# Output projection of a hybrid decoder layer: eight products of quarters replaced by seven (Strassen, Winograd's form)

## Chip, cores and metric

One core of a Trainium2 chip runs the kernel. The metric is the device time of one execution in microseconds (us); lower is better. The text calls the engines by the profile's names: PE is TensorE (PEld its weight loads), DVE is VectorE, ACT is ScalarE, POOL is GpSimd, SP is the engine whose queue issues every DMA.

## The reference

One decoder layer on a sequence of 1024 tokens with 1024 features, in float32. Three groups of heads work side by side; their gated results are concatenated to `y` (1024 x 1024) and projected by `w_out` (1024 x 1024). The result is normalized over its 1024 features, gated and added to the input:

```python
h = rmsnorm(x, g_pre) * (1.0 + scale[:, None]) + shift[:, None]
proj = h @ w_in
...
y_m = mlstm_branch(...) * jax.nn.silu(mz)
y_a = swa_branch(aq, ak, av, a_sinks) * jax.nn.silu(az)
y_s = stickbreak_branch(sq, sk, sv) * jax.nn.silu(sz)
y = jnp.concatenate([y_m, y_a, y_s], axis=-1) @ w_out
return x + gate[:, None] * rmsnorm(y, g_post)
```

## The kernel before, in words

Products that need float32 accuracy are made with split operands. `split` (L68) copies a float32 tile to a high part in the matmul's own format (ACT, L70) and subtracts to get a low part (DVE or POOL, L71). A product then takes three matmuls: high x high, low x high, high x low. `hh` and `hl` hold the high and low parts of the feature-major input, eight chunks `k` of 128 features by 1024 tokens. For most of the kernel that input is `h`, which the 128-feature blocks of the input projection read (`ProjD`, L359). These blocks are also the filler: `fill` issues their matmuls one by one between the steps of the mLSTM, the sliding window and the stick-breaking attention, so that PE always has something to do. The last of the blocks are the gates `z`.

`gated` (L468) handles a gate block when it is complete. It takes the sigmoid (ACT), multiplies the block by the group's result (DVE, L473), then by the sigmoid (POOL, L484, one step later), and one step after that (`rest`) splits the finished 128 x 512 piece of `y` and stores both parts in DRAM (`d_yh`, `d_yl`, L482 and L483). Chunks 6 and 7 (the stick-breaking heads) stay in SBUF (`ys`) and are split late, straight into `hh` and `hl`.

When the attention is done its SBUF is given back and the output stage begins (L1068). `wo_load` (L1072) loads a 128 x 1024 row block of `w_out` and splits it into `woh` and `wol`; `y_load` (L1077) runs the late splits of one half of the tokens and loads the stored parts of `y` back into `hh` and `hl`, over the old input, as soon as the last gate block has read it. `out_mm` (L1102) does one chunk for a 128-token row tile `i` and a half `n` of the columns, three matmuls of 128 x 512 into one PSUM bank (L1107 to L1109). Four row tiles advance together over seven chunks (eight banks), then they are completed one by one, and the other four row tiles follow, each over all eight chunks. `out_fin` (L1111) finishes a row tile: squares with a sum (ACT, L1120), multiplication by the gate row `gbc` from PSUM (DVE, L1122 and L1125), the power -1/2 (POOL, L1124), and per half a last operation with the reloaded `x` (DVE, L1128) and a store.

PE's order is that of the program text (`manual_schedule`, L74). The order on DVE, ACT, POOL and SP is chosen when the kernel is built, from program order and the readiness that the build's own timing gives; at run time each engine and SP's queue runs strictly in that order. Buffers rotate per tag (`bufs`): a new tile of a tag waits until the last reader of the tile that had the buffer is done.

Of the kernel before, what the change touches and what calls it, by code (L numbers as in the profile page):

```python
# [10 lines left out]
F32 = mybir.dt.float32  # L11
F32R = mybir.dt.float32r
# [34 lines left out]
def trunk(ctx: ExitStack, tc, x, w_ss, w_gate, rows, cols, w_mu, w_mif, w_dm, w_av, wqk, bif, alibi, w_out,  # L47
# [61 lines left out]
    d_yh, d_yl = dram("d_yh", [KT, P, S]), dram("d_yl", [KT, P, S])  # L109

    h_stk = ExitStack()
    hp = pool("ht", stack=h_stk)
# [355 lines left out]
    def gated(dst_j, name):  # L468
        def f(ps, n, t, src):
            sg = gst.tile([P, 512], F32, tag="gs", bufs=2, name=f"gs_{name}{n}")  # L470
            A.activation(sg, ps, AF.Sigmoid)
            y = src
            V.tensor_tensor(out=y, in0=ps, in1=src, op=ALU.mult)  # L473
# [10 lines left out]
            later(1, lambda: G.tensor_tensor(out=y, in0=y, in1=sg, op=ALU.mult))  # L484
            later(2, rest)
        return f
# [578 lines left out]
    ka_stk.close()  # L1065


    wop = pool("wop", side="right", stack=g_stk)  # L1068
    woh = wop.tile([P, KT, D], F32R, name="woh")
    wol = wop.tile([P, KT, D], F32R, name="wol")  # L1070

    def wo_load(k):  # L1072
        w = wop.tile([P, D], F32, tag="wo", bufs=2, name=f"wo{k}")
        load(w, w_out[k])
        split(woh[:, k, :], wol[:, k, :], w, A.copy, V if k % 2 else G)

    def y_load(n):  # L1077

        t = slice(n * 512, (n + 1) * 512)
# [20 lines left out]
    pso = {}  # L1100

    def out_mm(i, n, k):  # L1102
        t, cs = slice(i * P, (i + 1) * P), slice(n * 512, (n + 1) * 512)
        if k == 0:
            pso[i, n] = fbank(f"op{i}_{n}") if i % 4 == 3 else ops_.tile([P, 512], F32, tag="op", name=f"op{i}_{n}")
        o = pso[i, n]
        T.matmul(o, hh[:, k, t], woh[:, k, cs], start=(k == 0), stop=False)  # L1107
        T.matmul(o, hl[:, k, t], woh[:, k, cs], start=False, stop=False)  # L1108
        T.matmul(o, hh[:, k, t], wol[:, k, cs], start=False, stop=(k == KT - 1))  # L1109

    def out_fin(i):  # L1111
        t = slice(i * P, (i + 1) * P)
        xr = op_.tile([P, D], F32, tag="xr", bufs=2, name=f"xr{i}")
        load(xr, x[t, :])
        st = op_.tile([P, 4], F32, tag="st", bufs=2, name=f"st{i}")
        ot = op_.tile([P, D], F32, tag="ot", bufs=2, name=f"ot{i}")
        for n in range(2):
            cs = slice(n * 512, (n + 1) * 512)
            sj = op_.tile([P, 512], F32, tag="sj", bufs=2, name=f"sj{i}_{n}")
            A.activation(sj, pso[i, n], AF.Square, accum_out=st[:, n:n + 1])  # L1120
            if n == 0:
                V.tensor_tensor(out=ot[:, cs], in0=pso[i, n], in1=gbc[:, cs], op=ALU.mult)  # L1122
        V.tensor_scalar(out=st[:, 2:3], in0=st[:, 1:2], scalar1=st[:, 0:1], scalar2=D * EPS, op0=ALU.add, op1=ALU.add)  # L1123
        G.tensor_tensor(out=st[:, 3:4], in0=st[:, 2:3], in1=mhalf[:, 0:1], op=ALU.pow)  # L1124
        V.tensor_tensor(out=ot[:, 512:D], in0=pso[i, 1], in1=gbc[:, 512:D], op=ALU.mult)  # L1125
        for n in range(2):
            cs = slice(n * 512, (n + 1) * 512)
            V.scalar_tensor_tensor(out=ot[:, cs], in0=ot[:, cs], scalar=st[:, 3:4], in1=xr[:, cs], op0=ALU.mult,  # L1128
                                   op1=ALU.add)
            store(out[t, cs], ot[:, cs])  # L1130
        del pso[i, 0], pso[i, 1]

    for k in range(KT - 1):
        for i in range(4):
            for n in range(2):
                out_mm(i, n, k)
    for i in range(NT):
        for n in range(2):
            for k in ([KT - 1] if i < 4 else range(KT)):
                out_mm(i, n, k)  # L1140
        out_fin(i)
    for stack in (o_stk, g_stk, h_stk, fps_stk):
        stack.close()

# [47 lines left out]
```

## Time and profile before

| | |
|---|---|
| median of 3 runs | 552.52 us (552.3 to 553.77) |
| the profiled execution | 553.0 us, span 551.2 us |
| mean granted PE clock | 0.997 |
| PE busy | 523.9 us, 95%, 2953 matmuls |
| DVE busy | 332.5 us, 60% |
| ACT busy | 250.3 us, 45% |
| POOL busy | 220.6 us, 40% |
| three groups of output matmuls (L1107, L1108, L1109) | 128 each |

Busy times are of the one profiled execution. Matmuls overlap in the pipeline, so the duration of a row on PE is longer than the step from one matmul to the next. An arrow `<-` in a row's last field names what ended the idle time before it. A row of DMA on `SPq` is the time of its issue, not of its transfer.

### The profile page before, as it was taken

What the parts mean: (1) busy time and instruction counts of PE and PEld (TensorE: products, weight loads), DVE (VectorE), ACT (ScalarE), POOL (GpSimd) and SP (SyncE); (2) the same over time, 40 slices, a digit from 0 to 9 for tenths busy, and PEclk for the clock granted to TensorE, in tenths of its full rate; (3) what the DMA queues carried; (4) which work ended last, traced back from release to release, by engine and by line L of the source; (5) the groups of instructions that cost most, each with busy time, mean ns of one, the idle gap of its engine ahead of it and who ended that gap; (6) DMA issues with size and microseconds to landing.
All of it is one profiled execution on the core that took longest, in us unless ns stands there. A gap on an engine that the chain in (4) does not pass through costs nothing.

```text
span 551.2 us, 8550 instructions
## 1 busy us (share of the span) xinstructions
PE 523.9 (95%) x2953; PEld 449.0 (81%) x2953; DVE 332.5 (60%) x750; ACT 250.3 (45%) x571; POOL 220.6 (40%) x206
## 2 busy tenths in 40 slices
PE   4799999999998999999998999899999999999995
PEld 3577899899987989888786888788888888888884
DVE  4686692053707887678887479787878442108232
ACT  5643533451113333267677568667668432213100
POOL 2365765420033343234534348574766433111000
PEclk9999999999999999999999999999999999999998
DMA  8982360247986455699843389455421169607421
GB/s 307 417 293 75 120 227 21 59 145 219 284 240 222 135 162 125 162 268 299 238 150 98 125 226 249 142 149 167 134 77 59 39 193 404 238 5 238 144 84 69
DMA packets 63659, 96.57 MB, mean 175 GB/s; under 512 B 17600, under 2 KB 36992, under 8 KB 63488
## 3 DMA queue, kind: packets, MB, share of 16 engines
q1 hardware_dynamic: 63616, 96.03, 54.8%
q8 instruction: 23, 0.38, 0.3%
q14 instruction: 20, 0.16, 0.1%
HBM read 69.24 MB, written 25.20 MB: 171 GB/s over the span
## 4 chain that ended last, share of the span: by engine, by line
PE 78%; DVE 10%; DMA 4%; ACT 3%; issue 2%; POOL 2%; SPq 1%; DVEq 0%; POOLq 0%; ACTq 0%
PE pd L359 24%; PE ptav L385 6%; PE mu L233 6%; PE op L1109 5%; PE op L1108 5%; PE op L1107 5%; PE tp L994 3%; DMA ka<-d_akl 3%; PE ptmif L385 2%; DVE cu L509 2%; PE ops L1012 2%; PE ops L1013 2%; PE xps L166 2%; PE z L963 2%; PE mr L197 1%
## 5 line engine op out<-in xcount | busy, mean ns | idle before, releaser
L359 PE MATMUL pd<-hh,wl_d 128*128 128x512 f32 x256 | 71.1, 399 | 0.0
L359 PE MATMUL pd<-hh,wh_d 128*128 128x512 f32 x256 | 70.6, 400 | 0.0
L359 PE MATMUL pd<-hl,wh_d 128*128 128x512 f32 x256 | 70.6, 398 | 0.0
L302 POOL TENSOR_TENSOR wl_d<-w_d,wh_d 128x512 fp32r<-128x512 f32 x32 | 44.0, 1398 | 29.1 <-ACT wh_d L300 19.6
L359 PEld LDWEIGHTS pd<-hh,wh_d 128*128 128x128 f32 x256 | 46.1, 188 | 8.4 <-issue 0.5
L359 PEld LDWEIGHTS pd<-hl,wh_d 128*128 128x128 f32 x256 | 46.1, 188 | 8.0
L359 PEld LDWEIGHTS pd<-hh,wl_d 128*128 128x128 f32 x256 | 45.8, 188 | 7.7
L1108 PE MATMUL op<-woh,hl 128*128 128x512 f32 x128 | 50.6, 396 | 0.0
L1109 PE MATMUL op<-wol,hh 128*128 128x512 f32 x128 | 50.6, 396 | 0.0
L1107 PE MATMUL op<-woh,hh 128*128 128x512 f32 x128 | 50.6, 396 | 0.0
L982 POOL TENSOR_TENSOR sg<-sg,pr 128x512 f32<-128x512 f32 (+1 forms) x30 | 31.1, 1041 | 20.8 <-DVE pr L980 20.6
L857 POOL TENSOR_SCALAR zb<-zb,mx 128x256 f32<-128x256 f32 (+1 forms) x24 | 21.6, 914 | 42.5 <-DVE mx L854 28.4
L70 ACT CAST ah<-tp 128x512 fp32r<-128x512 f32 (+2 forms) x56 | 24.3, 436 | 29.2 <-PE tp L994 20.8
L71 DVE TENSOR_TENSOR al<-tp,ah 128x512 fp32r<-128x512 f32 (+2 forms) x56 | 27.4, 493 | 16.7 <-ACT ah L70 16.0
L1120 ACT ACTIVATE sj<-op 128x512 f32<-128x512 f32 x16 | 9.5, 597 | 50.4 <-PE op L1109 47.9
L1109 PEld LDWEIGHTS op<-wol,hh 128*128 128x128 f32 x128 | 24.0, 188 | 5.9
L1108 PEld LDWEIGHTS op<-woh,hl 128*128 128x128 f32 x128 | 24.0, 188 | 5.8
L1107 PEld LDWEIGHTS op<-woh,hh 128*128 128x128 f32 x128 | 24.0, 188 | 5.8
L1124 POOL TENSOR_TENSOR st<-st,mhalf 128x1 f32<-128x1 f32 x8 | 4.4, 554 | 57.5 <-DVE st L1123 57.5
L847 ACT ACTIVATE zb<-zb,mx 128x256 f32<-128x256 f32 (+1 forms) x48 | 23.2, 488 | 7.8 <-PE az L823 6.6
L980 DVE TENSOR_TENSOR_SCAN pr<-z,mzero 128x128 f32<-128x128 f32 (+3 forms) x32 | 25.6, 815 | 0.6 <-ACT z L971 0.2
L969 ACT ACTIVATE sg<-z 128x512 f32<-128x512 f32 (+3 forms) x48 | 23.8, 496 | 1.3 <-PE z L966 1.1
(247 smaller groups left out, 1328.4 us busy)
## 6 DMA issues: line engine op xcount, KB each, us to landing
wm<-in_w_ss_dram SPq DMA_DIRECT2D x16, 512.0 KB, 7.7
w_d<-in_w_dm_dram SPq DMA_DIRECT2D x16, 512.0 KB, 3.8
xt<-in_x_dram SPq DMA_DIRECT2D x8, 512.0 KB, 7.8
wg<-in_w_gate_dram SPq DMA_DIRECT2D x8, 512.0 KB, 5.8
wo<-in_w_out_dram SPq DMA_DIRECT2D x8, 512.0 KB, 5.2
xr<-in_x_dram SPq DMA_DIRECT2D x8, 512.0 KB, 4.7
out_dram<-ot SPq DMA_DIRECT2D x16, 256.0 KB, 2.3
hh<-d_yh SPq DMA_DIRECT2D x12, 256.0 KB, 6.0
```

What stands on the lines that cost most here:

```text
L70: e_hi(dst_h, src)
L71: e_lo.tensor_tensor(out=dst_l, in0=src, in1=dst_h.bitcast(F32), op=ALU.subtract)
L233: T.matmul(mu_acc[j][n], w[:, cs], h[:, k, t], start=(k == 0 and w is wh and h is hh), stop=(k == KT - 1 and h is hl))
L302: G.tensor_tensor(out=wl[:, a:b], in0=z[:, a:b], in1=wh.bitcast(F32)[:, a:b], op=ALU.subtract)
L359: T.matmul(ps, w[:, k, :], h[:, k, t], start=(k == 0 and w is wh and h is hh), stop=(k == KT - 1 and h is hl))
L385: T.matmul(ps[:, 0:self.N], h[:, k, t], w[:, k % 2, :], start=(k == 0 and q == 0), stop=(k == KT - 1 and q == 2))
L969: A.activation(sg[:, 0:w], zps[:, 0:w], AF.Sigmoid)
L980: V.tensor_tensor_scan(out=rev(pr), data0=rev(zps), data1=mzero[:, 0:1].to_broadcast([P, w]), initial=1.0 if nxt is None else nxt, op0=ALU ...
L982: (G if w > 256 and (h > 0 or i > 3) else V).tensor_tensor(out=sg[:, 0:w], in0=sg[:, 0:w], in1=pr[:, 1:w + 1], op=ALU.mult)
L1107: T.matmul(o, hh[:, k, t], woh[:, k, cs], start=(k == 0), stop=False)
L1108: T.matmul(o, hl[:, k, t], woh[:, k, cs], start=False, stop=False)
L1109: T.matmul(o, hh[:, k, t], wol[:, k, cs], start=False, stop=(k == KT - 1))
```

## The change

Tokens, columns and features are halved. Write Y(i,r) for token half i and feature half r of `y`, and W(r,n) for feature half r and column half n of `w_out`; a quarter is 512 x 512, four chunks of 128. The eight products Y(i,r) W(r,n) become seven, in this order of the code, with sums made in float32 ahead of the split:

- "1": Y(0,0) W(0,0), and "2": Y(0,1) W(1,0); their sum is the first output quarter
- "7": (Y(0,0) - Y(1,0)) (W(1,1) - W(0,1)); the factors are `yc` and `wc`
- "6": the next `yc` = Y(1,1) - `yc`, and `wc` = W(0,0) + `wc`
- "5": S1 = Y(0,0) + `yc` and T1 = W(1,1) - `wc`
- "3": the next `yc` = Y(0,1) - `yc`, with W(1,1)
- "4": Y(1,1), with `wc` - W(1,0)

`product` does 4 row tiles of 4 chunks and 3 passes, 48 matmuls, into four PSUM banks, and calls `evac` after each row tile. The parts p1 to p4 add the banks into SBUF rows. There are two high/low buffers for weight quarters, so a product's weights go into the buffer of the product two places earlier. The summed `y` quarters overwrite `hh`/`hl` quarters whose product is over. For this `y` is also stored in float32 (`d_y`); the high and low parts of chunks 0 to 3 of the second token half are no longer stored. The quarters are loaded several times, in 128 x 512 pieces of 256 KB with four buffers each for `w_out` and for `y`. `op_`, PSUM and the finish of a row (tiny operations, gate, last operation, store) are otherwise as before, but gates and last operations now read SBUF only, and two of the four output quarters are multiplied by the gate on POOL.

```diff
@@ gated / rest
                 if dst_j >= 6:
                     late[n].append(lambda: split(hh[:, dst_j, t], hl[:, dst_j, t], y, A.copy, V))
+                    return
+                store(d_y[dst_j, :, t], y)
+                if n == 1 and dst_j < 4:
                     return
@@ output stage
+    wq_, LOE = {}, (G, V)
+    def w_quarter(r, n, c):
+        z = wop.tile([P, 512], F32, tag="wo", bufs=4, name=f"wo{r}{n}{c}")
+        load(z, w_out[4 * r + c][:, halves[n]])
+        return z
+    def y_quarter(i, r, c):
+        if r == 1 and c >= 2:
+            return ys[:, c - 2, halves[i]]
+        z = wop.tile([P, 512], F32, tag="yo", bufs=4, name=f"yo{i}{r}{c}")
+        load(z, d_y[4 * r + c][:, halves[i]])
+        return z
+    def w_ready(name, chunk):
+        h, l = (wop.tile([P, 4, 512], F32R, tag=z, bufs=2, name=f"{z}{name}") for z in ("wqh", "wql"))
+        for c in range(4):
+            split(h[:, c, :], l[:, c, :], chunk(c), A.copy, LOE[c % 2])
+        wq_[name] = (h, l)
+    def y_ready(i, r, chunk):
+        for c in range(4):
+            k = 4 * r + c
+            split(hh[:, k, halves[i]], hl[:, k, halves[i]], chunk(c), A.copy, LOE[c % 2])
+    def summed(dst, a, b, op):
+        V.tensor_tensor(out=dst, in0=a, in1=b, op=op)
+        return dst
...
-        for k in range(6):
+        for k in range(4 * n, 6):
             load(hh[:, k, t], d_yh[k, :, t])
             load(hl[:, k, t], d_yl[k, :, t])
-    for k in range(4):
-        wo_load(k)
+    w_ready("1", lambda c: w_quarter(0, 0, c))
     fill.through(I_SZ1)
     y_load(0)
-    for k in range(4, KT):
-        wo_load(k)
+    w_ready("2", lambda c: w_quarter(1, 0, c))
+    for c in range(4):
+        summed(yc(c), y_quarter(0, 0, c), y_quarter(1, 0, c), ALU.subtract)
+        summed(wc(c), w_quarter(1, 1, c), w_quarter(0, 1, c), ALU.subtract)
     fill.through(99)
     y_load(1)
+    y_ready(1, 0, yc)
...
+    def product(yi, yr, w, evac):
+        ps = banks(f"p{w}_")
+        wh, wl = wq_[w]
         for i in range(4):
+            t = slice(yi * 512 + i * P, yi * 512 + (i + 1) * P)
+            for c in range(4):
+                k = 4 * yr + c
+                T.matmul(ps[i], hh[:, k, t], wh[:, c, :], start=(c == 0), stop=False)
+                T.matmul(ps[i], hl[:, k, t], wh[:, c, :], start=False, stop=False)
+                T.matmul(ps[i], hh[:, k, t], wl[:, c, :], start=False, stop=(c == 3))
+            evac(i, ps[i])
...
+    def finish(i, parts):
+        s_ = st[:, i, :]
+        V.tensor_scalar(out=s_[:, 2:3], in0=s_[:, 1:2], scalar1=s_[:, 0:1], scalar2=D * EPS, op0=ALU.add, op1=ALU.add)
+        G.tensor_tensor(out=s_[:, 3:4], in0=s_[:, 2:3], in1=mhalf[:, 0:1], op=ALU.pow)
+        for n, o, gate in parts:
+            if gate:
+                V.tensor_tensor(out=o, in0=o, in1=gbc[:, halves[n]], op=ALU.mult)
+        for n, o, _ in parts:
+            V.scalar_tensor_tensor(out=o, in0=o, scalar=s_[:, 3:4], in1=xrs[i][:, halves[n]], op0=ALU.mult, op1=ALU.add)
+            store(out[i * P:(i + 1) * P, halves[n]], o)
+    def p1(i, ps):
+        A.copy(u1[i], ps)
+    def p2(i, ps):
+        V.tensor_tensor(out=o11[i], in0=ps, in1=u1[i], op=ALU.add)
+        square(o11[i], i, 0)
+        G.tensor_tensor(out=o11[i], in0=o11[i], in1=gbc[:, halves[0]], op=ALU.mult)
+    def p7(i, ps):
+        V.tensor_tensor(out=u2[i], in0=ps, in1=u1[i], op=ALU.add)
+    def p6(i, ps):
+        V.tensor_tensor(out=u2[i], in0=ps, in1=u2[i], op=ALU.add)
+        V.tensor_tensor(out=u1[i], in0=ps, in1=u1[i], op=ALU.add)
+    def p5(i, ps):
+        V.tensor_tensor(out=o22[i], in0=ps, in1=u2[i], op=ALU.add)
+        V.tensor_tensor(out=u1[i], in0=ps, in1=u1[i], op=ALU.add)
+        square(o22[i], 4 + i, 1)
+        G.tensor_tensor(out=o22[i], in0=o22[i], in1=gbc[:, halves[1]], op=ALU.mult)
+    def p3(i, ps):
+        x_again(i)
+        V.tensor_tensor(out=u1[i], in0=ps, in1=u1[i], op=ALU.add)
+        square(u1[i], i, 1)
+        finish(i, ((0, o11[i], False), (1, u1[i], True)))
+    def p4(i, ps):
+        x_again(4 + i)
+        V.tensor_tensor(out=u2[i], in0=u2[i], in1=ps, op=ALU.subtract)
+        square(u2[i], 4 + i, 0)
+        finish(4 + i, ((0, u2[i], True), (1, o22[i], False)))
+    product(0, 0, "1", p1)
+    w_ready("7", wc)
+    product(0, 1, "2", p2)
+    y_ready(0, 0, lambda c: summed(yc(c), y_quarter(1, 1, c), yc(c), ALU.subtract))
+    w_ready("6", lambda c: summed(wc(c), w_quarter(0, 0, c), wc(c), ALU.add))
+    product(1, 0, "7", p7)
...
+    y_ready(0, 1, s1)
+    w_ready("5", t1)
+    product(0, 0, "6", p6)
+    y_ready(1, 0, lambda c: summed(yc(c), y_quarter(0, 1, c), yc(c), ALU.subtract))
+    w_ready("3", lambda c: w_quarter(1, 1, c))
+    product(0, 1, "5", p5)
+    w_ready("4", lambda c: summed(wc(c), wc(c), w_quarter(1, 0, c), ALU.subtract))
+    product(1, 0, "3", p3)
+    product(1, 1, "4", p4)
```

`s1` and `t1` load Y(0,0) and W(1,1) again and add or subtract `yc` and `wc`.

More of the change, by code (lines that the diff above doesn't have):

```diff
@@ L108, in trunk @@
     d_ym, d_ya = dram("d_ym", [3, P, S], F32), dram("d_ya", [3, P, S], F32)
-    d_yh, d_yl = dram("d_yh", [KT, P, S]), dram("d_yl", [KT, P, S])
+    d_yh, d_yl = dram("d_yh", [6, P, S]), dram("d_yl", [6, P, S])
+    d_y = dram("d_y", [6, P, S], F32)
     h_stk = ExitStack()
@@ L1068, in trunk @@
     wop = pool("wop", side="right", stack=g_stk)
[L1069 to L1075, printed above, removed]
+    ysum = wop.tile([P, 4, 512], F32, name="ysum")
+    wsum = wop.tile([P, 4, 512], F32, name="wsum")
+    halves = (slice(0, 512), slice(512, 1024))
+    wq_, LOE = {}, (G, V)
[21 more added lines that the diff above has]
+        return dst
+    wc, yc = lambda c: wsum[:, c, :], lambda c: ysum[:, c, :]
     def y_load(n):
-        t = slice(n * 512, (n + 1) * 512)
+        t = halves[n]
         for _ in range(3):
@@ L1099, in trunk @@
     ops_ = pool("ops", bufs=6, space=PSUM, stack=o_stk)
[L1100 to L1131, printed above, removed]
@@ L1133, in trunk, with banks, rows_of @@
-    for k in range(KT - 1):
-        for i in range(4):
[L1135 to L1141, printed above, removed]
+    def banks(name):
+        return [fbank(f"{name}{i}") if i == 3 else ops_.tile([P, 512], F32, tag="op", name=f"{name}{i}")
+                for i in range(4)]
+    def rows_of(name):
+        return [op_.tile([P, 512], F32, tag=name, bufs=4, name=f"{name}{i}") for i in range(4)]
@@ new lines, in trunk, with square, x_again @@
+    u1, u2, o11, o22 = (rows_of(z) for z in ("u1", "u2", "o11", "o22"))
+    st = op_.tile([P, NT, 4], F32, name="st")
+    def square(src, i, n):
+        sj = op_.tile([P, 512], F32, tag="sj", bufs=2, name=f"sj{i}_{n}")
+        A.activation(sj, src, AF.Square, accum_out=st[:, i, n:n + 1])
+    xrs = {}
+    def x_again(i):
+        xrs[i] = op_.tile([P, D], F32, tag="xr", bufs=2, name=f"xr{i}")
+        load(xrs[i], x[i * P:(i + 1) * P, :])
+    def finish(i, parts):
[8 more added lines that the diff above has]
+            store(out[i * P:(i + 1) * P, halves[n]], o)
```

6 lines of the change are left out of this document (added).

## The prediction

> **What bounds the kernel now.** I read the page's busy strip first, then the table of stretches over the end of the run, then the order-of-time view of each engine there.
>
> The strip (40 slices of 13.8 us, busy tenths) and the shares of the chain, from the page:
>
> ```profile
> PE   4799999999998999999998999899999999999995
> DVE  4686692053707887678887479787878442108232
> POOL 2365765420033343234534348574766433111000
> PEclk9999999999999999999999999999999999999998
> PE 78%; DVE 10%; DMA 4%; ACT 3%; issue 2%; POOL 2%; SPq 1%; DVEq 0%; POOLq 0%; ACTq 0%
> ```
>
> Three stretches of 11.2 us in the last stage (length, then busy us of PE, weight loads, DVE, ACT and POOL, each with its instructions, granted clock, DMA share, GB/s):
>
> ```profile
> 455.20:466.40 11.20, 11.20 (x50) 9.01 (x48) 3.81 (x5) 3.83 (x5) 3.94 (x3) 1.00 1.05 405
> 466.40:477.60 11.20, 11.20 (x50) 9.02 (x48) 1.03 (x1) 2.10 (x2) 2.25 (x1) 1.00 0.71 278
> 522.40:533.60 11.20, 11.20 (x50) 9.02 (x48) 2.92 (x5) 1.38 (x4) 0.55 (x1) 1.00 0.28 94
> ```
>
> The stage's first and last matmul and what follows the last one, in order of time (start, duration):
>
> ```profile
> 455.19 0.40 PE L1107 MATMUL op<-woh,hh 128*128 128x512 f32 x1
> ...
> 544.56 0.40 PE L1109 MATMUL op<-wol,hh 128*128 128x512 f32 x1
> 545.06 0.60 ACT L1120 ACTIVATE sj<-op 128x512 f32<-128x512 f32 x1 [4.84 <-PE op L1109]
> 545.78 0.21 DVE L1123 TENSOR_SCALAR st<-st 128x1 f32<-128x1 f32 x1 [4.83 <-ACT sj L1120]
> 546.13 0.55 POOL L1124 TENSOR_TENSOR st<-st,mhalf 128x1 f32<-128x1 f32 x1 [10.65 <-DVE st L1123]
> 546.72 1.42 DVE L1128 SCALAR_TENSOR_TENSOR ot<-ot,st,xr 128x512 f32<-128x512 f32 x2
> ```
>
> TensorE (PE) is full to the end and holds 78% of the chain. In the output projection it is alone: of 11.20 us VectorE (DVE), ScalarE (ACT) and GpSimd (POOL) use 1 to 4 (third, fourth and fifth pair of figures in a stretch's row). The stage has 384 matmuls; the first starts at 455.19, the last at 544.56, so the step is 89.37 / 383 = 0.2333 us (the 0.40 us of a row is the pipelined duration, not the step). After the last start, 6.6 us pass until the span ends at 551.2: square, two tiny operations, two final operations, a store.
>
> **Matmuls removed.** 7 products of 4 row tiles, 4 chunks and 3 passes are 336. 48 fewer at 0.2333 us: **-11.2 us**, all on the path. One product then takes 48 steps, 11.2 us, a row tile 2.8 us, and without any wait the last matmul would be over at about 533.6.
>
> **What each piece costs on its engine.** The prices come from the same operations elsewhere in the trace: first the groups (count, busy us, mean ns, idle before), then two meetings of VectorE and GpSimd in order of time, then one of another kind.
>
> ```profile
> L71 POOL TENSOR_TENSOR sl_az<-d_ya_92r,sh_az 128x512 fp32r<-128x512 f32 x6 | 7.7, 1289 | 4.6 <-ACT sh_az L70 4.6
> L484 POOL TENSOR_TENSOR d_ya_92r<-d_ya_92r,gs_az 128x512 f32<-128x512 f32 x6 | 7.7, 1286 | 0.0
> L70 ACT CAST hh<-ys 128x512 fp32r<-128x512 f32 x4 | 2.5, 622 | 8.9 <-PE pd L359 4.6 <-POOL ys L484 4.3
> L1120 ACT ACTIVATE sj<-op 128x512 f32<-128x512 f32 x16 | 9.5, 597 | 50.4 <-PE op L1109 47.9
> ```
> ```profile
> 449.80 2.77 DVE L71 TENSOR_TENSOR hl<-ys,hh 128x512 fp32r<-128x512 f32 x1 [3.94 <-PE pd L359]
> 452.49 0.68 DVE L473 TENSOR_TENSOR ys<-pd,ys 128x512 f32<-128x512 f32 x1
> 453.09 1.21 DVE L71 TENSOR_TENSOR wol<-wo,woh 128x1024 fp32r<-128x1024 f32 x1
> 449.62 2.40 POOL L71 TENSOR_TENSOR wol<-wo,woh 128x1024 fp32r<-128x1024 f32 x1 [3.37 <-ACT woh L70]
> 453.25 2.20 POOL L484 TENSOR_TENSOR ys<-ys,gs_sz 128x512 f32<-128x512 f32 x1 [1.23 <-DVE ys L473]
> ```
> ```profile
> 427.41 2.53 POOL L302 TENSOR_TENSOR wl_d<-w_d,wh_d 128x512 fp32r<-128x512 f32 x2
> 427.60 0.69 DVE L473 TENSOR_TENSOR d_ya_92r<-pd,d_ya_92r 128x512 f32<-128x512 f32 x1 [0.41 <-ACT gs_az L471]
> ```
>
> A GpSimd tensor operation on 128x512 is 1.29 us, a VectorE one starts its successor 0.60 us later (452.49 to 453.09), a split's ScalarE copy is 0.62 us. ScalarE has, after 455.2, nine splits of four copies, two or three late ones and four evacuations, some 43 at 0.62, and 16 squares at 0.60: 36 us beside 78 us of products, taken as nothing; should a copy come late, its split waits for it, which the upper ends below include.
>
> The second fence decides more. A VectorE operation with both inputs in SBUF (449.80) that meets a GpSimd operation (449.62 to 452.02) takes 2.77 us and ends at 452.57, 0.55 us after the other. In reverse, the GpSimd one of 453.25 ends at 455.45, 1.15 us after VectorE's 453.09 to 454.30. They take turns. The third fence is the exception: with one input in PSUM (`pd`) VectorE keeps its 0.69 us beside a busy GpSimd. So I charge one shared ledger, 0.55 us for a VectorE operation with two SBUF inputs, 1.15 for a GpSimd one, and leave VectorE's 32 additions from PSUM (32 x 0.60 = 19.2 us) outside it, to run under GpSimd's time.
>
> Without the turns the same work would be 69 us on VectorE (62 x 0.60 + 11.4 + 19.2 + 1.7) and 42 on GpSimd (29 x 1.29 + 4.4), by the counts below; neither would bind, and the sum would be near -8. The Trainium skill (SBUF — State Buffer, "Who interferes with whom") states the turns as an exclusive lock, held for the whole instruction, and exempts a VectorE operation with at most one SBUF input; by that rule, which all three pairs of rows bear out, the sum is the one below.
>
> **The ledger, product by product.** In code order, with g for GpSimd and s for two-SBUF VectorE operations, after 455.2:
> - product 1: last gating 1g, late splits 2s, W2 split 2g 2s, the eight differences 8s, first y split 2g 2s: 5g 14s, 13.4 us
> - product 2: split "7" 2g 2s, gate multiply 4g, y sum and split 2g 6s, w sum 4s: 8g 12s, 15.8
> - product 7: split "6" 2g 2s; S1 and its split 2g 6s, T1 4s: 4g 12s, 11.2
> - product 6: split "5" 2g 2s, y sum and split 2g 6s: 4g 8s, 9.0
> - product 5: split "3" 2g 2s, w sum 4s, gate multiply 4g: 6g 6s, 10.2
> - products 3 and 4: split "4" 2g 2s, eight gate multiplies 8s, sixteen final operations of 0.71 (half of 1.42)
>
> Together 29g, 62s and 16 x 0.71: 33.4 + 34.1 + 11.4 = 78.9 us, and the eight `pow` at 0 to 0.55 each, of which I take half: **81 us against 78.4 us of products**. The idle engines of the old stage become a full pair.
>
> **Waits between products.** A product's weight buffers are free only when the product two places earlier has ended. Due before product 6 (ideal start 488.8): 13.4 + 15.8 + 3.4 = 32.6 of 33.6 us, if the pair never starves. It starves a little at first:
>
> ```profile
> hh<-d_yh SPq DMA_DIRECT2D x12, 256.0 KB, 6.0
> 449.76 0.63 SPq L64 DMA_DIRECT2D hh<-d_yh  x1
> 450.59 0.37 SPq L64 DMA_DIRECT2D hl<-d_yl  x1
> 452.28 0.32 SPq L64 DMA_DIRECT2D hh<-d_yh  x1
> 452.95 0.32 SPq L64 DMA_DIRECT2D hl<-d_yl  x1
> 444.50 1.72 SPq L64 DMA_DIRECT2D wo<-in_w_out_dram  x2
> ```
>
> The queue starts at 444.50. Ahead of product 7 stand 16 d_yh/d_yl loads, 8 of W1 and W2 and 16 for the differences: 40 of 256 KB at a 0.67 us step (452.28 to 452.95), which is also what 405 GB/s carries: until about 471. The differences follow the loads, so "7" and the first y split are ready near 474, before 477.6: no wait there, but 1 to 3 us of pair time lost. Product 6 comes 0 to 2 us late; I take 1. Before product 5: 4g 12s remain, 11.2 of 11.2 us, and product 6's eight additions (4.8) only partly fit under 4.6 us of GpSimd: 0 to 3 late; I take 1.5. Product 3 needs 4g 8s, 9.0; product 4 needs 2g 6s, 5.6: no wait. **+2.5 us**; ends 0 and 15 (1.29 and 0.60 for every entry, and no addition hidden).
>
> Product 1 itself needs the fourth pair of y chunks at its tenth matmul, 455.2 + 9 x 0.233 = 457.3. That pair was issued at 449.76 and 450.59 and lands 6.0 later, 456.6: covered by 0.7 us; without cover +1. Each later load has at least a product's time.
>
> **The tail.** A row of products 3 and 4 costs VectorE 0.60 (from PSUM) + 0.21 + 0.60 (gate) + 1.42 = 2.83 us, and TensorE gives a row every 2.80. Nothing is caught up. What VectorE still owes when product 3 begins stays to the end: split "4" (1.1), the last additions of product 5 (1.2), its waits for four or so GpSimd turns (4.6, half of it under additions: 2.3), together 4.6; the last row's own latencies hide about half a microsecond of it: **+4**. The last row also passes through one more addition before its square: **+0.7**. Ends for the tail: 0.7 and 12 (w sum and every `pow` late as well).
>
> **Ahead of the projection.** 8 of the 24 d_yh/d_yl stores go, with 4 copies and 4 GpSimd differences; 12 d_y stores come: 4 more on SP's queue, and each gated tile is held until its store has read it.
>
> ```profile
> 300.00:444.30 144.30, 141.02 (x809) 121.09 (x808) 104.95 (x215) 95.03 (x213) 83.44 (x72) 1.00 0.44 131
> ```
>
> TensorE is busy 141 of 144 us there and DMA at 0.44: taken as nothing; a changed order on the other engines can move it a microsecond either way.
>
> **Sum.** -11.2 + 2.5 + 4 + 0.7 = **-4.0 us**. The profiled execution took 553.0 (551.2 and 1.8 around it): 549.0. The median of the runs, 552.5, is 0.5 below it, so for the median I forecast **548.5**, with 545 to 550.8 as this case's own range.
>
> **Rivals.**
> *The pair is the bound (slower).* The ledger of 81 us begins at 455.2 and a store of about 3 us follows it, as 546.72 + 1.42 to 551.2 shows. Used to 90% it ends at 455.2 + 90 + 3.1 = 548.3; to 85%, 553.6; to 83%, 555.9. Below 87% the change loses. For it: in-order queues, splits that wait for copies, the full ledger. Against: VectorE alone has 69 us and much of the work is ready early. At 83%: +4.7, 557.
>
> *The pair packs well.* No waits, and the tail only 0.7 to 3: -10.5 to -7, 542 to 545.5. For it: work can run a product ahead where buffers allow.
>
> *Given back entirely.* Waits and tail together cost 9.5 to 12.9 against the 11.2: 550.8 to 554.2, not to be told from no change, as 0.3% (1.7 us) is about what a measurement of this kernel can tell. For it: half the distance between the forecast's 7.2 and the upper ends. Against: both terms would have to be some 40% larger than the ledger gives.
>
> *A wait long enough to lose the clock (slower).*
>
> ```profile
> 547.00:548.00 1.00, 0.00 (x0) 0.00 (x0) 1.00 (x2) 0.00 (x0) 0.00 (x0) 1.00 0.00 0
> 548.00:549.00 1.00, 0.00 (x0) 0.00 (x0) 0.13 (x1) 0.00 (x0) 0.00 (x0) 0.70 0.65 248
> 549.00:550.00 1.00, 0.00 (x0) 0.00 (x0) 0.00 (x0) 0.00 (x0) 0.00 (x0) 0.50 0.71 277
> ```
>
> The granted clock halves at about 548.4, some 3.4 us after the last matmul. If one product waits over 3.4 us, its first matmuls run at half clock; if that lasts as long as the fall took, 1.7 us are lost on top: two such waits and the tail give -11.2 + 2 x 5.1 + 4.7 = +3.7, 556. The Trainium skill (TensorE: Matmul & The Clock Gate, Part 1) gives about 3.4 us for both directions; the fall agrees with the rows, the return no row here shows.
>
> **Chances.** Forecast 0.48; packs well 0.12; given back 0.15; the pair as bound 0.20; lost clock 0.05. So faster 0.60, same 0.15, slower 0.25. The range runs from the packed case to the pair at 83%: 542.5 to 557.
>
> **What would show it.** Right: 336 `op`-like matmuls with a 0.233 step inside a product; gaps on TensorE, if any, at the starts of products 6 and 5, ended by GpSimd or VectorE splits; VectorE and GpSimd at seven tenths and more between them from 460 on; VectorE operations of 1.5 us and more beside GpSimd ones; VectorE busy without a pause over the last 10 us and a tail of 9 to 12 us after the last matmul. Wrong: a gap before product 2 or 7 ended by a load (the queue is the bound), a tail under 8 us, or gaps above 8 us together.

## The result and the profile after

| | before | after |
|---|---|---|
| median of 4 runs | 553.12 us (552.30 to 553.77) | 567.71 us (565.92 to 568.92) |
| the profiled execution | 553.0 us, span 551.2 us | 568.3 us, span 566.6 us |
| mean granted PE clock | 0.997 | 0.977 |

The ratio after to before is 1.026, 95% interval 1.023 to 1.030: the change makes the kernel slower by 2.6%. The forecast was 548.5 us, its range ended at 557. (The median before that stands ahead of the prediction, 552.52 us, is of three of these four runs.)

First the page of the changed kernel, the rows that stand in the prediction for the kernel before:

```profile
PE   4799999999989999998999998999999998669990
DVE  5777690146438787687885598877875446999886
POOL 2356664510133434163433465736655345553721
PEclk9999999999999999999999999999999999688996
PE 64%; DVE 17%; DMA 7%; issue 4%; POOL 3%; ACT 3%; SPq 1%; POOLq 0%; DVEq 0%; ACTq 0%
```

Each slice is 14.2 us. Up to slice 34 PE reads much as before. In slices 35 and 36 it is busy for six tenths, the granted clock falls in the same place, and DVE, whose last slices read 2 1 0 8 2 3 2 before, now reads 9 9 9 8 8 6.

The stretches of the last stage (columns as in the prediction):

```profile
455.00:477.00 22.00, 21.76 (x92) 16.94 (x91) 10.42 (x14) 10.26 (x21) 9.26 (x8) 1.00 1.01 377
477.00:488.00 11.00, 4.84 (x15) 2.94 (x14) 11.00 (x11) 4.73 (x9) 7.45 (x5) 0.75 0.66 209
488.00:499.00 11.00, 10.29 (x36) 7.71 (x36) 11.00 (x14) 5.13 (x9) 5.43 (x4) 0.78 0.48 162
499.00:510.00 11.00, 6.31 (x21) 4.45 (x20) 11.00 (x12) 4.77 (x8) 6.50 (x5) 0.84 0.24 84
510.00:521.00 11.00, 11.00 (x42) 8.73 (x42) 11.00 (x17) 3.51 (x7) 3.40 (x4) 0.85 0.24 72
```

The third pair of figures is DVE. In the first 22 us it works less than half the time. Then it is busy for 44 us without a pause (11.00 of 11.00, four times), while POOL has room. An engine that is full beside a PE at 4.84 or 6.31 of 11 is the first to suspect. What PE waited for in the products (us in total, times, longest):

```profile
PE p L1155 <- DVE wql L71: 5.7, 4, 4.3
PE p L1153 <- ACT wqh L70: 4.4, 1, 4.4
PE p L1155 <- POOL wql L71: 1.5, 1, 1.5
PE p L1154 <- DMA hl<-d_yl: 0.2, 1, 0.2
```

Together 11.8 us, half of it for DVE itself; the copy on ACT is followed further below.

PE in order of time: the first matmul of the products, those behind the longer gaps, the last one.

```profile
454.79 0.40 PE L1153 MATMUL p<-wqh,hh 128*128 128x512 f32 x1
...
479.52 0.50 PE L1155 MATMUL p<-wql,hh 128*128 128x512 f32 x1 [0.25 <-DVE wql L71]
484.40 0.79 PE L1153 MATMUL p<-wqh,hh 128*128 128x512 f32 x1 [4.37 <-ACT wqh L70]
487.16 0.79 PE L1155 MATMUL p<-wql,hh 128*128 128x512 f32 x1 [1.54 <-POOL wql L71]
489.52 0.80 PE L1155 MATMUL p<-wql,hh 128*128 128x512 f32 x1 [0.71 <-DVE wql L71]
...
507.43 0.79 PE L1155 MATMUL p<-wql,hh 128*128 128x512 f32 x1 [4.30 <-DVE wql L71]
...
552.17 0.40 PE L1155 MATMUL p<-wql,hh 128*128 128x512 f32 x1
```

From the first start to the last are 97.38 us, where 335 steps of 0.2333 would be 78.16: 19.2 us too many. All 336 starts are in the trace. Seven steps are longer than 0.62 us and hold 13.6 us of the excess: one in product 1 (a load, 0.5), four at the start of product 7, two in product 6. Twenty-three more steps, all behind the two waits of over four microseconds, are of 0.42 to 0.59 us, at half clock: 5.1 us. From the last matmul's start to the end of the span are 14.4 us (before: 6.6).

The DVE groups of this stage, with the idle time in front of them in the last field:

```profile
L71 DVE TENSOR_TENSOR wql<-wsum,wqh 128x512 fp32r<-128x512 f32 x6 | 6.1, 1020 | 0.3 <-ACT wqh L70 0.2
L1180 DVE SCALAR_TENSOR_TENSOR u<-u,st,xr 128x512 f32<-128x512 f32 x8 | 6.0, 748 | 4.0 <-DMA xr<-in_x_dram 3.5 <-POOL st L1175 0.4
L71 DVE TENSOR_TENSOR wql<-wo,wqh 128x512 fp32r<-128x512 f32 x6 | 5.4, 914 | 2.9 <-ACT wqh L70 2.9
L1108 DVE TENSOR_TENSOR wo<-wo,wsum 128x512 f32<-128x512 f32 x4 | 4.6, 1146 | 0.0
L1187 DVE TENSOR_TENSOR o<-p,u 128x512 f32<-128x512 f32 x4 | 2.8, 688 | 4.6 <-PE p L1155 4.6
L1206 DVE TENSOR_TENSOR u<-p,u 128x512 f32<-128x512 f32 x4 | 2.7, 683 | 0.0
L71 DVE TENSOR_TENSOR hl<-ys,hh 128x512 fp32r<-128x512 f32 x3 | 2.0, 690 | 3.9 <-ACT hh L70 3.9
```

Sums and splits with both inputs in SBUF (`wsum`, `wo`) take 0.9 to 1.15 us on the mean; the additions from PSUM (`p`) take 0.68 to 0.69. Where DVE was idle, it stood for the copies of the late splits and of W2 (3.9 and 2.9 us), for PE ahead of the additions of product 2 (4.6 us), and in the tail for rows of `x` (3.5 us).

How one wait of product 7 comes about, all engines in order of time:

```profile
479.39 0.68 DVE L1187 TENSOR_TENSOR o<-p,u 128x512 f32<-128x512 f32 x1
479.60 1.27 POOL L71 TENSOR_TENSOR hl<-ysum,hh 128x512 fp32r<-128x512 f32 x1 [1.28 <-ACT hh L70]
479.99 1.43 DVE L1108 TENSOR_TENSOR ysum<-yo,yo 128x512 f32<-128x512 f32 x1
480.96 1.58 POOL L1189 TENSOR_TENSOR o<-o,gbc 128x512 f32<-128x512 f32 x1
481.35 1.75 DVE L1108 TENSOR_TENSOR ysum<-ys,ysum 128x512 f32<-128x512 f32 x1
483.02 0.68 DVE L1108 TENSOR_TENSOR wsum<-wo,wo 128x512 f32<-128x512 f32 x1
483.73 0.62 ACT L70 CAST wqh<-wsum 128x512 fp32r<-128x512 f32 x1
484.40 0.79 PE L1153 MATMUL p<-wqh,hh 128*128 128x512 f32 x1 [4.37 <-ACT wqh L70]
```

PE waits for the ACT copy of 483.73, which waits for the third sum of W7 (483.02). In front of that sum in DVE's queue stand two sums of `y` that product 7 doesn't need at this point (the first is for its last chunk, the second for product 6). They take 1.43 and 1.75 us in place of 0.68; POOL's operations of 479.60 and 480.96 run beside them. The addition of 479.39 does run beside the POOL operation of 479.60, as the prediction had it, but for half a microsecond; the next two-input operation then waits out the rest.

### The profile page after: what moved, and what is told of

Same layout as the page of the kernel before. It is cut to its first block, busy times and chain, and to the rows that moved or that the text cites. A ratio compares the mean times of both kernels' runs of the same rounds, so it can differ in the third digit from the quotient of the medians.

```text
span 566.6 us, 8680 instructions
## 1 busy us (share of the span) xinstructions
PE 519.8 (92%) x2905; PEld 442.6 (78%) x2905; DVE 391.5 (69%) x824; ACT 268.3 (47%) x607; POOL 251.9 (44%) x228
## 4 chain that ended last, share of the span: by engine, by line
PE 64%; DVE 17%; DMA 7%; issue 4%; POOL 3%; ACT 3%; SPq 1%; POOLq 0%; DVEq 0%; ACTq 0%
PE pd L360 23%; PE ptav L386 6%; PE mu L234 6%; PE tp L998 3%; PE ptmif L386 2%; DVE cu L513 2%; PE p L1155 2%; PE p L1154 2%; PE ops L1016 2%; PE p L1153 2%; PE ops L1017 2%; PE xps L167 2%; PE z L967 1%; PE mr L198 1%; DMA d_kl<-sl_sk 1%
## 5 line engine op out<-in xcount | busy, mean ns | idle before, releaser
L1155 PE MATMUL p<-wql,hh 128*128 128x512 f32 x112 | 47.1, 421 | 7.2 <-DVE wql L71 5.7
L1153 PE MATMUL p<-wqh,hh 128*128 128x512 f32 x112 | 46.5, 416 | 4.4 <-ACT wqh L70 4.4
L1154 PE MATMUL p<-wqh,hl 128*128 128x512 f32 x112 | 46.3, 413 | 0.2 <-DMA hl<-d_yl 0.2
L1155 PEld LDWEIGHTS p<-wql,hh 128*128 128x128 f32 x112 | 22.2, 198 | 15.0 <-DVE wql L71 7.7
L1153 PEld LDWEIGHTS p<-wqh,hh 128*128 128x128 f32 x112 | 22.4, 200 | 10.2 <-ACT wqh L70 4.7
L1154 PEld LDWEIGHTS p<-wqh,hl 128*128 128x128 f32 x112 | 22.3, 199 | 6.2 <-DMA hl<-d_yl 0.7
L975 ACT ACTIVATE z<-z 128x512 f32<-128x512 f32 (+3 forms) x48 | 24.0, 500 | 0.0
L301 ACT CAST wh_d<-w_d 128x1024 fp32r<-128x1024 f32 x16 | 16.8, 1048 | 13.8 <-PE pd L360 9.5
```

Source lines behind the costliest of these rows:

```text
L975: A.activation(zps[:, 0:w], zps[:, 0:w], AF.Sigmoid, scale=-1.0)
L1153: T.matmul(ps[i], hh[:, k, t], wh[:, c, :], start=(c == 0), stop=False)
L1154: T.matmul(ps[i], hl[:, k, t], wh[:, c, :], start=False, stop=False)
L1155: T.matmul(ps[i], hh[:, k, t], wl[:, c, :], start=False, stop=(c == 3))
```

## The experiments

Two theories at the start. *Turns and one queue*: DVE, with its operations lengthened by its turns with POOL, is one in-order chain from 455 us to the end, and PE waits on it. *Loads*: the sums of product 7 come late because SP's queue, with four buffers each, brings the quarters late. A third was *order*: there is work enough done in time, only in the wrong order.

Each kernel of this section was timed once, `e11` and `e12` four times. The four runs of the changed kernel lie 3.0 us apart (565.92 to 568.92), so a difference of two or three microseconds from its median can be chance. With every edit the build also chooses the order on DVE, ACT, POOL and SP anew.

**POOL made to read nothing** (`e3`). Half of the low parts are zeros that POOL writes without reading, and the two gate multiplications on POOL are left out.

```diff
-            split(h[:, c, :], l[:, c, :], chunk(c), A.copy, LOE[c % 2])
+            part(h[:, c, :], l[:, c, :], chunk(c), c)   # c even: A.copy(h, src); G.memset(l, 0.0)
...
-        G.tensor_tensor(out=o11[i], in0=o11[i], in1=gbc[:, halves[0]], op=ALU.mult)
...
-        G.tensor_tensor(out=o22[i], in0=o22[i], in1=gbc[:, halves[1]], op=ALU.mult)
```

> GpSimd's part of the product stage reads no SBUF any more (but for the eight small powers): its low parts are set to zero instead of being differences, and its two multiplications by the gate row are left out. VectorE's operations are unchanged. Theory 'turns': VectorE's two-SBUF operations of 1.7 us go back to 0.68, product 6 waits under 1 us, the tail after the last matmul shrinks from 14 to 8 to 10 us, while product 7 still waits 5 us or more for its loads; time 553 to 558. Rival 'VectorE by itself': it has too much work with or without turns; product 6 still waits over 3 us, time 563 to 567.

Measured: 555.32 us, 12.4 below the changed kernel. DVE over the whole stage, first the changed kernel, then this one:

```profile
455.00:567.00 112.00, 85.77 (x336) 65.86 (x334) 89.75 (x120) 39.15 (x80) 49.69 (x37) 0.88 0.58 201
```
```profile
455.00:567.00 112.00, 82.53 (x339) 65.09 (x338) 71.15 (x119) 37.56 (x78) 17.02 (x26) 0.92 0.58 202
```

And two of its groups on DVE:

```profile
L1115 DVE TENSOR_TENSOR wo<-wo,wsum 128x512 f32<-128x512 f32 x4 | 2.7, 677 | 0.0
L1211 DVE TENSOR_TENSOR u<-p,u 128x512 f32<-128x512 f32 x4 | 2.7, 684 | 0.1
```

The same 120 operations take 71.2 us in place of 89.8. The sums shown fall from 1.15 to 0.68 us, the additions from PSUM stay as they were. The difference, 18.6 us, is the turns: 28 POOL operations that read SBUF are left out or only write here (20 subtractions, 8 multiplications), some 0.66 us of DVE for each. PE's waits fall from 11.8 to 3.2 us, all in product 7. The theory of turns holds, and the time lies in its range. The edit also makes POOL's low parts ready early; as PE waited only 1.5 us for one of them in the changed kernel, that can't be the 12.4. Two of the expectations missed: product 7 was to wait 5 us or more, and the tail was to shrink to 8 to 10. It stayed at 13.1 us, of which 4.8 are waits for rows of `x`.

**All low parts on DVE** (`e6`). `LOE = (V, V)` in place of `(G, V)`: POOL keeps only gates and powers.

> All low parts of the splits on VectorE, none on GpSimd: 26 more subtractions of about 0.6 us on VectorE, and nothing of GpSimd beside them but the gates and the powers. Theory (each GpSimd subtraction costs VectorE about its own length, 0.7 to 1.1 us, in turns): the VectorE operations fall back to 0.6 to 0.7 us each and the sum stays as it was or falls a little: 563 to 569 us. Rival (GpSimd really takes work off VectorE, and only the long operations of 1.75 us look bad): 26 x 0.6 = 16 us more on the chain less half of it hidden, 575 us or more.

Measured: 563.96 us, 3.8 below the changed kernel's median and 2.0 below its fastest run. In the same stage DVE does 20 operations more and is busy 2.3 us less:

```profile
455.00:564.00 109.00, 83.37 (x340) 65.06 (x338) 87.43 (x140) 39.43 (x78) 20.28 (x17) 0.88 0.60 208
```

POOL gave no help here: taking a subtraction over costs DVE no more than the turn that it saves. The last matmul starts at 543.82, 8.4 us earlier, but the tail is 18.4 us, 6.0 of it waits for rows of `x`: what DVE no longer owes in the middle it owes at the end. The time is what the theory expected; the rival's 575 is far off.

**Loads and order.** `e1` gives the quarters of `w_out` and of `y` eight buffers each in place of four; `e2` runs the first three chunks of products 1, 2, 7, 6 and 5 over all four row tiles before the last chunk, so that a product needs its later weights later; `e5` does both.

```diff
-        z = wop.tile([P, 512], F32, tag="wo", bufs=4, ...)      # e1, and the same for "yo"
+        z = wop.tile([P, 512], F32, tag="wo", bufs=8, ...)
...
+        for c in range(lead):                                   # e2; lead = 3, and 0 for "3" and "4"
+            for i in range(4):
+                mm(i, c)
         for i in range(4):
+            for c in range(lead, 4):
+                mm(i, c)
```

> Eight buffers instead of four for the loaded quarters of w_out and of y; nothing else. Theory 'load chain': product 7 waits because the differences are fed by four buffers, each of which is loaded again only after the split or the sum that read it, behind the d_yh and d_yl loads; the waits inside product 7 (7.7 us in all) fall below 2 us, the granted clock stays at 1.00 there, and the time falls by 7 to 10 us, to 558 to 561. Rival 'pair': VectorE and GpSimd are too busy to make the factors in time; the loads come earlier but the sums do not, product 7 still waits 6 us or more, and the time stays at 565 to 569.

> Products 1, 2, 7, 6 and 5 run chunks outermost (chunks 0 to 2 for all four row tiles, then chunk 3 row by row), so that chunk c is needed 2.8 c us after the start of the product instead of 0.7 c. Theory 'latency': the factors come late by a few us only; product 7 waits some 3 us in place of 7.7, product 6 under 1 in place of 5, the clock does not fall, time 556 to 559. Rival 'throughput': what PE does not wait for in products 7 and 6 it waits for in 5 and 3, or VectorE carries it into the tail, which grows from 14 to over 18 us; time 562 to 566.

> Both eight buffers and chunks outermost. 'Load chain' plus 'latency': no product waits over 1 us, the clock stays at 1.00, the matmuls take 79 to 81 us, and only the tail of 12 to 16 us is left: 551 to 555. If the pair is the bound in throughput: waits move to products 5 and 3 or into the tail, 557 to 562.

Measured: 564.45, 569.08 and 566.27 us. `e1` lies between its two theories, 3.3 us below the changed kernel's median and 1.5 below its fastest run; `e2` and `e5` lie above both of their ranges and within 1.5 us of that median. More buffers do bring the work forward: in `e1` DVE works 15.11 of the first 22 us in place of 10.42. But PE still waits 10.2 us, half of it in product 7 and half in products 6 and 5. The order won nothing that these runs show: in `e2` PE still waits 10.0 us, of which the longest is 4.5. The last matmul starts at 549.40, 549.49 and 549.77, although the first one of `e5` comes only at 457.75. Over the stage DVE is busy 92.0 us in `e2` and 91.0 in `e5`, against 89.8 in the changed kernel: the waits move, and DVE's queue gets no shorter.

**Rows of `x`** (`e4`). Four buffers in place of two.

```diff
-        xrs[i] = op_.tile([P, D], F32, tag="xr", bufs=2, name=f"xr{i}")
+        xrs[i] = op_.tile([P, D], F32, tag="xr", bufs=4, name=f"xr{i}")
```

> Four buffers in place of two for the rows of x in the tail; they are now fetched before the weight loads of the last product instead of between the last outputs. Theory (VectorE is one chain, of which two waits of the tail for rows of x, 3.5 us together, are a part): 3 to 4 us less, 564 to 565 us, no wait for a row of x after the last matmul. Rival (rows of x only hide another wait of the tail, for the squares, the power or the stores): within 1.5 us of the changed kernel's 567.7.

Measured: 565.71 us, 2.0 below the median, but only 0.2 below the fastest run of the changed kernel, so a gain is not shown. No wait for `x` is left, but the tail is 13.7 us in place of 14.4. The last matmul started 2 us earlier; how an earlier fetch of `x` did that was not followed up.

**The sums of `w_out` made early.** The factors T of products 7, 6, 5 and 4 depend on `w_out` alone. `e7` makes and splits them early (planned for 80 to 130 us; the trace has them from 78 to 150), stores both parts in DRAM, and the end stage only fetches them; `e8` does so for the plain quarters too. In both the fourth sum reads the second one after its split has put the low part in its place, so T of product 4 has other values; the instructions are those of the right sum. `e9` and `e10` pace the early work (eight half-size units, loads two units ahead, a step after every 16 matmuls of the filler) with the sums in order. `e8`, `e9` and `e10` also have eight buffers for the quarters of `y` and four for the rows of `x`.

```diff
+            A.copy(h, t)                                        # early, for T of 7, 6, 5, 4
+            V.tensor_tensor(out=t.bitcast(F32R), in0=t, in1=h.bitcast(F32), op=ALU.subtract)
+            store(d_th[name][c], h)
+            store(d_tl[name][c], t)
...
-    w_ready("7", wc)                                            # the end stage
+    w_fetch("7")                                                # loads d_th, d_tl into wqh, wql
```

> The four sums of quarters of w_out and their splits are worked out early (80 to 130 us, where VectorE is busy under 6 of 10 us), kept in DRAM, and only fetched in the end. It takes 16 sums and 16 splits out of the end stage, 24 of VectorE's operations there, 8 of GpSimd's and 16 of ScalarE's. Theory (VectorE with its turns is the chain): 24 x 0.6 plus 8 turns of about 1 us = 22 us less on it, of which the matmuls, at 67 us, let about 15 be seen: 545 to 556 us. Rival 1 (the waits of product 7 come from the loads, which are no fewer): 560 to 566 us. Rival 2 (the early work itself delays the front by as much): the first product's matmul comes later than 456 us, and the time is above 560 us.

> As e7_hoist, with the three plain quarters' splits worked out early too, so that no work on w_out is left in the end stage, and with eight buffers for the quarters of y and four for the rows of x. VectorE keeps 32 additions from PSUM, 16 sums of y, 10 low parts, the gates and the outputs: about 32 x 0.62 + 16 x 0.65 + 10 x 0.6 + 24 x 0.65 = 52 us plus turns, below the matmuls' 67 us. Theory: TensorE sets the pace again, waits under 3 us in all and the granted clock stays whole; first matmul 455 + 67 + 3, tail 10 to 13 us, 538 to 546 us, below the 552.5 of the kernel before. Rival (the end stage then waits for transfers: 14.7 MB of weights' parts in place of 7.3): gaps of product 7 end by a load, and 550 us or more.

> The early sums of e7_hoist again, but paced: in eight half-size units, the loads two units ahead of their sums and each unit's stores a step behind its splits, one step after every 16 matmuls of the filler, so that neither the DMA queue nor VectorE stands waiting in front of what the front of the kernel needs; eight buffers for the quarters of y and four for the rows of x. In e7_hoist the stage from the first product's matmul to the end took 573.2 - 481.0 = 92.2 us (before: 95.7), and the front came 25.8 us late. Theory (VectorE's chain was what made the change slow, and the front's lateness was the queue's): first product's matmul between 455 and 458 us, stage 90 to 93 us, 546 to 552 us. Rival (12 MB more of transfers and 32 more VectorE operations delay the front whatever their order): first product's matmul at 462 us or later, and 555 us or more.

> As e9_hoist_paced, with the low parts that are left in the end (three plain quarters of w_out, the quarters of y) all on VectorE as in e6_low_on_v. Theory (TensorE sets the pace of this stage now, and VectorE has 25 us of slack): within 1.5 us of e9_hoist_paced, with the long VectorE operations gone. Rival (turns still set the tail): 2 us or more below e9_hoist_paced.

Measured: 575.02, 609.57, 581.44 and 582.06 us. The first three are 19 to 64 us above the ranges of their theories, all of it lost ahead of the end stage, as the rivals of `e7` and `e9` had it; `e10` is within 1.5 us of `e9`, as expected. The first matmul of the products came at 481.0, 516.6, 487.3 and 488.7 in place of 454.8. PE's longest gap in the front, of `e7` and then of `e9`:

```profile
175.88 2.08 PE L590 MATMUL gbps<-gacc,ones 128*128 128x512 f32 x2 [15.65 <-DVE gacc L581]
```
```profile
139.68 0.69 PE L386 MATMUL ptav<-wh_av,hh 128*128 128x384 f32 x1 [19.53 <-ACT wh_av L301]
```

In `e7` the sum over the gate's weights is late, whose loads SP issues from 151.5 us on in place of 125.1 in the kernel before, with new stores ahead of them in its order. In `e9` it is the split of the next weights on ACT, and behind it SP again: the load of `w_av` is issued at 132.87 in place of 101.43 in the changed kernel, among the new loads and stores, and the copy at 138.80 stood 2.1 us for it. So DVE may have had room at that place; the in-order queues between there and PE had none. That the order of SP's queue alone would mend it was not tried. The end stages answer to the theory, though: from the first product's matmul to the end 92.2, 91.2, 92.3 and 91.6 us, where the changed kernel has 111.8 and the kernel before 96.0 (551.2 - 455.2; the 95.7 in the expectations is a slip). Low parts on DVE changed nothing in `e10`, as expected once DVE has slack. A late front could also have let the loads run ahead, so the short stage alone doesn't decide; the next two runs do.

**The end stage alone.** In `e11` the parts of T are not made at all; the end fetches as many bytes of other data as `e7` fetches of T. `e12` treats the three plain quarters in the same way, puts the low parts of `y` on DVE, and has eight buffers for the quarters of `y` and four for the rows of `x`.

```diff
+            load(h[:, c, :], d_qh[c % 2][:, halves[c // 2]])    # in w_fetch
+            load(l[:, c, :], d_ql[c % 2][:, halves[c // 2]])
```

> The end stage of e7_hoist with nothing paid ahead of it: the four sums of quarters of w_out are not worked out at all; in their place the end fetches as many bytes of other rounded data (the parts of q, written by 200 us), so the output is not the reference's. It prices the stage alone. Theory (VectorE's chain made the change slow; with 24 operations less on it TensorE sets the pace and the 48 matmuls' saving comes through, less the longer tail): first product's matmul at 455 us, 92 us to the end as in e7_hoist, 547.2 + 1.7 = 549 us, 0.6% faster than the kernel before. Rival (the stage of e7_hoist was short only because the late front let the loads run ahead): gaps of product 7 come back, 553 us or more.

> As e11_sums_given with the three plain quarters given as well (no work on w_out in the end), the low parts of y on VectorE, eight buffers for the quarters of y and four for the rows of x; the output is not the reference's. VectorE keeps some 90 operations of 0.6 to 0.7 us. Theory (what is left above 455 + 78.4 is the tail and two waits at product 2 and 7): tail 9 to 11 us, 544 to 548 us. Rival (the tail is a chain per row tile that no relief of VectorE shortens, 11 to 14 us): the same as e11_sums_given within 1 us.

Measured: `e11` 549.76 us, ratio to before 0.995 (0.993 to 0.996); `e12` 549.37, ratio 0.993 (0.991 to 0.995). `e11` came out at the 549 of the theory, with a stage of 92.0 us (547.4 - 455.4) as in `e7`, though its front is on time. Its waits on PE, its DVE over the stage, and one group there:

```profile
PE p L1159 <- DVE hl L71: 0.9, 1, 0.9
PE p L1158 <- DMA wqh<-d_qh: 0.3, 1, 0.3
```
```profile
455.00:549.00 94.00, 79.83 (x339) 63.07 (x337) 62.59 (x96) 29.89 (x64) 37.23 (x30) 0.95 0.76 272
```
```profile
L1211 DVE TENSOR_TENSOR u<-p,u 128x512 f32<-128x512 f32 x4 | 2.7, 685 | 1.5 <-PE p L1160 1.5
```

With 24 operations fewer DVE is busy 27.2 us less (16.3 of their own; the rest, by subtraction, in turns), the additions shown now wait for PE, and PE waits 1.2 us. The products run from 455.38 to 535.75, 2.2 us over the 78.16. Of the saving of 11.2 us these 2.2 go, and 5.1 more to the tail, 11.7 us against 6.6. In `e12` the tail is down to 8.1 us, but the weights of product 7 arrive late (2.8 us of waits for loads). Its profiled run, 547.07 us, was the fastest of four; by the median, above the 544 to 548 of its theory, it isn't told from `e11`. That is what its rival said, though not for the rival's reason, a tail that stays at 11 to 14.

## Why the prediction was wrong

| step | predicted | measured, profiled executions |
|---|---|---|
| matmuls removed | -11.2 us | -11.2 (336, 299 of 335 steps at full rate) |
| ahead of the projection | 0 | -0.4 (454.79 for 455.19) |
| waits between products | +2.5 | +13.6, and +5.6 for the clock and small steps |
| the tail | +4.7 | +7.8 (14.4 for 6.6) |
| sum | -4.0 | +15.4 |

**Right**: the matmuls and their step, nothing ahead of the projection, the turns themselves (operations of 1.5 us and more beside POOL's; 69 us of VectorE's own work forecast without turns, 71.2 measured), and that additions from PSUM keep their length. The Trainium skill (SBUF — State Buffer, "Who interferes with whom") has the shared port as an exclusive lock: outside its two-port modes a DVE operation with at most one SBUF input doesn't contend with POOL, and one with two SBUF inputs contends only with a POOL operation that reads SBUF. The runs agree with both: the additions from PSUM take 0.68 to 0.69 us in the changed kernel and in `e3`, and the sums shown take 0.68 us in `e3`, where POOL writes zeros, in place of 1.15.

**The step that failed** is in "What each piece costs": the 32 additions from PSUM, 19.2 us, were left outside the ledger, "to run under GpSimd's time". In the trace of the changed kernel they are on VectorE for 20.8 us, and 6.8 of these lie beside one of GpSimd's 128x512 operations; 14.0 do not. An addition can only run there if it happens to be next in VectorE's queue while GpSimd has its turn. When the next one is a sum with two SBUF inputs, that sum waits at the head of the queue and the additions stand behind it. GpSimd's own entries erred the other way: at 1.15 us each they were 33.4 us of the ledger, and 28 of them cost VectorE 18.6. So the ledger should not have been one of the pair, but VectorE's own: all its operations (71.2 us, the busy time of `e3`) plus 0.66 us for each of the 28 (18.6), 89.8 us in place of the 81 of the ledger, against 78.4 of products. This sum is the measured busy time taken apart, not a test of it; the test is that the time fell when `e3` took the turns away and `e11` 24 of the operations.

**The second error** is in "Waits between products": "no wait there" for product 7, with 1 to 3 us of lost time at the start. VectorE had about 12 us of idle time up to 475 us: for the copies of late splits, for W2, and for PE in front of product 2's additions, which stood in its queue ahead of the sums of `w_out` (first one at 473.15). With 89.8 us of work and 18 of idle time, the chain that began at 455.4 ends at 563.1, and the last store makes it 566.6. Eight buffers (`e1`) took 4.7 us off the early idle time and at most some 3 us off the kernel, so the load chain was a part only. What each of the two errors cost in time was not measured apart.

**The rivals.** "The pair is the bound (slower)", at a chance of 0.20, named the mechanism and the side, and put it at 557, 11 us short. VectorE was busy for 89.8 of the 107.7 us of its chain, 83%; that this is the very figure of that rival is chance, since the rival's 83% was of a ledger 9 us too short. "A wait long enough to lose the clock", at 0.05, had the waits right: two of over four microseconds came, and the matmuls at half clock cost PE 5.1 us where the rival reckoned 3.4. That they cost the kernel any time is not shown. VectorE has no idle time from 476 to 525 and never waits for a matmul after 476; it comes to the additions of product 7's last two rows, which PE had ended by 499.9, only here:

```profile
513.07 1.28 DVE L1192 TENSOR_TENSOR u<-p,u 128x512 f32<-128x512 f32 x2
```

A PE at full clock would not have brought these forward. By the prediction's own signs, gaps above 8 us together were to show it wrong, and they did; the tail of 14.4 lies outside its 9 to 12. The gaps were ended by splits, as it had said, but in products 7 and 6 and not in 6 and 5; a gap before product 2 or 7 ended by a load, its sign against the queue, did not come.

**The tail** was taken as what VectorE still owed. That was half of it. Relieving VectorE alone (`e11`) brings it from 14.4 to 11.7 us, of which 2.3 are still waits for rows of `x`; four buffers for `x` alone (`e4`) bring it to 13.7. With both (`e9`, `e12`) it is 8.1. The waits for `x` were in no term of the forecast, which had VectorE busy without a pause at the end.

**What it could have been worth.** With all sums and splits of `w_out` given for nothing (`e12`) the change wins 0.7%. With this end stage, the work on `w_out` has therefore to be had for under 4 us anywhere else in the kernel; in the placements tried the first product came 26 to 62 us late.

## What to carry to other kernels

When a change trades TensorE's work for elementwise work, write the ledger of the busiest in-order queue alone: its own operations, plus a turn for each GpSimd operation that reads SBUF beside its two-input ones (here 0.66 us); don't count on operations that need no turn to slip past one that waits. GpSimd was no help to a VectorE that was already the chain: twenty subtractions moved from GpSimd to VectorE made VectorE's busy time shorter, 87.4 us for 89.8. And idle time of an engine is room for more work only if the queues before and behind it, SP's and ScalarE's here, have room as well.

## What the runs showed of the hardware

The granted clock after the wait that ended at 507.43:

```profile
508.00:510.00 2.00, 2.00 (x6) 1.59 (x5) 2.00 (x3) 1.67 (x3) 1.30 (x1) 0.50 0.32 121
510.00:512.00 2.00, 2.00 (x6) 1.51 (x6) 2.00 (x2) 0.78 (x2) 2.00 (x2) 0.50 0.02 4
512.00:514.00 2.00, 2.00 (x8) 1.58 (x7) 2.00 (x4) 0.62 (x1) 0.00 (x0) 0.68 0.45 117
514.00:516.00 2.00, 2.00 (x10) 1.60 (x9) 2.00 (x4) 0.00 (x0) 0.00 (x0) 1.00 0.06 21
```

PE is busy throughout, and the clock is whole again only at about 513.2 us, 5.8 us after the matmuls began again; the step is 0.43 us until then. The Trainium skill (TensorE: Matmul & The Clock Gate, Part 1) gives about 3.4 us of sustained activity, in a window that runs freely; this return took longer than one such window. After the earlier wait, matmuls between 484.40 and 489.52 were broken by two more gaps, and the clock came back 3.3 us after the last of them.

The power on one column took POOL 0.55 us in the kernel before and 0.93 in the changed one, in `e11` and in `e12`, whose DVE and POOL have less to do; the two differ in the tile (four columns of one row tile before, one tile for all row tiles after), and that this is the cause was not tried.
